# Layer 0 begins on a scale-only input: x transposed on the host, the shift added afterwards

## The chip, the cores and the metric

The kernel runs on one core of one Trainium2 chip. The metric is the time of one execution on the device in microseconds; the time given for a kernel is the median over its runs. A profile is one execution recorded by the hardware profiler, with every instruction's start and end.

## The reference

Two layers of a mixer that serves a context pass (128 rows, conditioned by `c_ctx`) and a denoising step (512 rows, conditioned by `c`) with the same weights. All data are float32. The part that matters here:

```
def layer_step(x, cvec, p, ...):
    shift, scale, gate = split(silu(cvec) @ w_ada + b_ada, 3)      # w_ada: 2048 x 6144
    h = rms_norm(x, norm_g) * (1.0 + scale) + shift                # x: 128 or 512 rows of 2048
    aq, ak, av, ag, bq, bff, bfb, bi, bg, cu, cv, cg = split_proj(h @ w_in)   # w_in: 2048 x 6656
    a_out = windowed attention of aq, ak, av (QK norm, rotary positions) * silu(ag)
    b_out = two gated linear recurrences (HGRN) of bq, bff, bfb, bi, normed * silu(bg)
    c_out = cu * (position mixing of layer-normed cv) * silu(cg)
    y = concat(a_out, b_out, c_out) @ w_out                        # 2048 x 2048
    return x + gate * y, ...
```

Returned are the final x of both passes, the context keys and values of each layer and the final states of the recurrences.

## The kernel before, in words

The 640 rows (128 of context, then 512 of the sample) make five row tiles (NT = 5), the 2048 columns sixteen slices k (KT = 16). For the big products h lies transposed in SBUF: for each k a tile of 128 columns of h by 640 rows. To multiply float32 exactly enough in the fast format, each operand is split into a high part and a rest (`hh`, `hl` for h, `wh`, `wl` for weights; ScalarE copies the high part, VectorE subtracts), and three matmuls per pair of tiles are added up in PSUM: wh with hh, wl with hh, wh with hl (L426 to L428 in row products, L443 in column products).

`rowmajor` makes 512 columns of `h @ W` for all five row tiles: for each k it loads 128 x 512 of W, splits it, and issues 15 matmuls of 512 columns into five PSUM banks (240 in all). `colmajor` makes 128 columns, transposed: for each k six matmuls, three of 384 and three of 256 rows (96 in all). A layer has five row products of `w_in` (AK with AV, AQ, AQ+512, BI, CV), 32 column products (BFF, BFB, BQ, BG, four each, AG eight, CU and CG four each) and four row products of `w_out`.

Side work hangs on the products. `tick()` advances the generators in `self.side` (key and query preparation, attention, recurrence, SGU) by one step between matmuls; `fill()` advances `ada_gen`, which makes the remaining w_ada columns on VectorE (two L286 operations per step) while the products run, at 1.25 steps a group in layer 0. A scheduler orders each engine's instructions ahead of time by a priority, which is the place in the program; what is issued under `hi()` counts as 3000 places earlier. Loads of weights go through SP's queue, x and most small loads through ScalarE's.

Layer 0 begins like this: x comes in rows through ScalarE's queue (`load_x`), ScalarE squares it for the norm (L354), `scale_x` multiplies it by the reciprocal root (L372, L374), and `make_h` transposes it on TensorE (L381, L386), applies scale and shift on VectorE (L388, L390) and splits it. Scale and shift of layer 0 come from `ada_first`, in four blocks of four k's: for each block, w_ada's 512 shift columns and 512 scale columns (8 MB) are loaded, thin matmuls with the two conditioning vectors (L242, 32 columns of weights side by side in four column groups) make them as rows, and small matmuls turn the rows into columns (L254). The first block comes ahead of the AK product; the other three are made during it, four k's ahead of their use.

Of the kernel before, what the change touches and what calls it, by code (L numbers as in the profile page):

```python
# [8 lines left out]
F32 = mybir.dt.float32  # L9
# [4 lines left out]
ALU = mybir.AluOpType  # L14
# [28 lines left out]
def host_consts():  # L43
# [25 lines left out]
    for qd in range(4):  # L69
        for cd in range(2):  # L70
            misc[32 * qd + cd, 248 + 2 * qd + cd] = 1.0
# [5 lines left out]
class Net:  # L77
    def __init__(self, ctx, tc, I, C, O):
        self.tc, self.nc, self.I, self.C, self.O = tc, tc.nc, I, C, O
        self.ctx = ctx  # L80
        self.pools()
        self.uid = 0

# [37 lines left out]

    def hi(self):
        return self.tc.high_priority(offset=HP)

    # ---------------------------------------------------------------- constants
    def setup(self):
# [8 lines left out]
        self.sel8 = misc[:, 248:256]  # L135
# [16 lines left out]
        self.sc = self.g(512).rearrange("p (k c) -> p k c", k=KT)  # L152
        nc.vector.memset(self.sc, 0.0)
        self.s2 = cst.tile([P, KT, 2], F32, name="s2")
        self.ones = cst.tile([P, 32], F32, name="ones")
# [31 lines left out]
    def setup2(self):  # L187
# [25 lines left out]
        self.gd = [self.dr.tile([2, D], F32, name=f"gd{l}", tag=f"gd{l}") for l in range(DEPTH)]  # L213
        self.x1 = [self.dr.tile([P, D], F32, name=f"x1_{t}", tag=f"x1_{t}") for t in range(NT)]
# [7 lines left out]
    # ---------------------------------------------------------------- adaLN  # L222
    def ada_load(self, blk, k, pool):
        raw = []
        with self.hi():
            for s in range(2):
                if pool == "hp":
                    r = self.hp.tile([P, 512], F32, tag=("hh", "hl")[s], name=self.nm("wa"))
                else:
                    r = self.ev(512)  # L230
                c0 = D * s + 512 * blk
                self.nc.sync.dma_start(r, self.I["w_ada"][0, k * P:(k + 1) * P, c0:c0 + 512])
                raw.append(r)
        return raw

    def ada_first(self, blk, pre):
        nc = self.nc
        acc = self.bank()
        for k in range(KT):
            raw = pre[k] if k < len(pre) else self.ada_load(blk, k, "hp")  # L240
            for qd in range(4):
                nc.tensor.matmul(  # L242
                    acc[32 * qd:32 * qd + 32, 0:256],
                    lhsT=self.sc[:, k, :],
                    rhs=raw[qd // 2][:, 256 * (qd % 2):256 * (qd % 2) + 256],
                    start=k == 0, stop=k == KT - 1, skip_group_check=True,
                )
            if k < KT - 1:
                yield
        rows = self.g(256)  # L250
        nc.scalar.activation(rows, acc[:, 0:256], AF.Copy)
        b = self.bank()
        for s in range(2):
            nc.tensor.matmul(b[:, 8 * s:8 * s + 8], lhsT=rows[:, 128 * s:128 * s + 128], rhs=self.sel8,  # L254
                             start=True, stop=True, skip_group_check=True)
        ps = b[:, 0:16].rearrange("p (s q c) -> p q s c", s=2, q=4)
        for qq in range(2):
            k0 = 4 * blk + 2 * qq
            self.mod_cols(0, 0, k0, 2, ps[:, qq])
            self.mod_cols(0, 1, k0, 2, ps[:, 2 + qq])  # L260
        yield

# [11 lines left out]
    def ada_steps(self, l, blk):  # L274
# [15 lines left out]
        if blk >= 8:  # L290
            for cd in range(2):
                nc.tensor.matmul(b[32 * cd:32 * cd + 32, :], lhsT=self.ones, rhs=acc[:, cd], start=True, stop=True,
                                 skip_group_check=True)
# [47 lines left out]
    # ---------------------------------------------------------------- layer input  # L341
    def load_x(self):
        self.xt = []
        self.ssq = self.small(4 * NT, "ssq")
        for t in range(NT):
            x = self.mg()
            src = self.I["x_prompt"][0] if t == 0 else self.I["x_sample"][0, (t - 1) * P:t * P]
            for c in range(4):
                self.nc.scalar.dma_start(x[:, 512 * c:512 * c + 512], src[:, 512 * c:512 * c + 512])
            self.xt.append(x)  # L350
        for t in range(NT):
            for c in range(4):
                junk = self.ev(512)
                self.nc.scalar.activation(junk, self.xt[t][:, 512 * c:512 * c + 512], AF.Square,  # L354
                                          accum_out=self.ssq[:, 4 * t + c:4 * t + c + 1])
# [43 lines left out]
    # ---------------------------------------------------------------- big products  # L399
    def wload(self, srcs, nk, n):  # L400
        nc = self.nc
        with self.hi():
            raw = self.wrp.tile([P, nk, n], F32, tag="wr", name=self.nm("wr"))
            o = 0
            for s in srcs:
                w = s.shape[1]
                nc.sync.dma_start(raw[:, :, o:o + w], s.rearrange("(a p) n -> p a n", p=P))
                o += w
# [6 lines left out]
    def rowmajor(self, W, c0, hook=None):  # L415
# [3 lines left out]
        for ks in groups:  # L419
            if hook is not None:  # L420
                hook(ks[0])
# [700 lines left out]
```

## Time and profile before

| what | value |
|---|---|
| median of three runs | 2324.17 us (2321.46 to 2326.08) |
| span of the profiled execution, first to last instruction | 2323.5 us |
| TensorE matmuls busy | 2230.3 us (96%) |
| VectorE busy | 1387.9 us (60%) |
| ScalarE busy | 763.2 us (33%) |
| GpSimd busy | 308.2 us (13%) |
| mean granted TensorE clock | 0.988 |
| moved by DMA | 283.70 MB, mean 122 GB/s |

The profiled execution has no time of its own besides its span, which is what the views are measured against; it stands 0.7 us under the median. "Busy" of TensorE is the union of its matmuls' records; these overlap, as the next begins before the one before has ended, so the distance between their starts says more than their length. Line numbers (L426) are those of the kernel before. A plain float32 matmul shows as two records.

### The profile page before, as it was taken

The numbers are of one execution on the slowest core, as the hardware profiler recorded it, in microseconds if no ns is written. First come the engines' busy times: TensorE is split into PE (matmuls) and PEld (weight loads), VectorE is DVE, ScalarE is ACT, GpSimd is POOL, SyncE is SP. The second block draws the span as 40 slices with busy tenths as digits, with TensorE's granted clock in tenths as the row PEclk, the third lists the DMA queues.
The fourth block names the chain that finished last, engine by engine and source line by source line (L and its number), as shares of the span: only waits on it lengthen the run. The fifth ranks groups of instructions, "written<-read, shape, count | busy, mean of one in ns | idle before, by whom it ended". The sixth has DMA issues, their size and how long they took to land.

```text
span 2323.5 us, 35038 instructions
## 1 busy us (share of the span) xinstructions
PE 2230.3 (96%) x13362; PEld 1960.9 (84%) x13362; DVE 1387.9 (60%) x2570; ACT 763.2 (33%) x1593; POOL 308.2 (13%) x242
## 2 busy tenths in 40 slices
PE   3999999999999999999999999999999999999999
PEld 1668778989989989988887878799999998998887
DVE  2367797688988768652236456855865942434232
ACT  4232344434333322242224234344343332223111
POOL 0011010022222101011112010101222310100110
PEclk9999999999999999999999999999999999999999
DMA  9864333344443555543332221322422423324332
GB/s 345 316 195 124 111 101 109 112 120 134 133 124 114 172 166 147 151 158 109 109 118 73 77 60 50 116 60 72 124 82 75 122 88 92 100 78 150 105 109 82
DMA packets 255612, 283.70 MB, mean 122 GB/s; under 512 B 17586, under 2 KB 156740, under 8 KB 254164
## 3 DMA queue, kind: packets, MB, share of 16 engines
q1 hardware_dynamic: 243664, 256.59, 35.7%
q10 hardware_dynamic: 11780, 24.88, 3.3%
q8 instruction: 105, 1.72, 0.3%
q14 instruction: 63, 0.52, 0.1%
HBM read 269.30 MB, written 12.09 MB: 121 GB/s over the span
## 4 chain that ended last, share of the span: by engine, by line
PE 80%; DVE 11%; DMA 5%; issue 2%; ACT 1%; POOL 0%; SPq 0%; DVEq 0%; ACTq 0%; POOLq 0%
PE m L443 32%; PE m L426 13%; PE m L427 13%; PE m L428 12%; DMA wa<-in_w_ada_dram 4%; DVE aacc L286 3%; DVE wl L412 2%; PE s L621 1%; PE s L667 1%; PE s L242 1%; DMA wr<-in_w_in_dram 1%; PE s L831 1%; PE s L679 1%; DVE g L507 1%; DVE g L508 1%
## 5 line engine op out<-in xcount | busy, mean ns | idle before, releaser
L412 DVE TENSOR_TENSOR wl<-wr,wh 128x512 fp32r<-128x512 f32 x544 | 404.6, 745 | 620.2 <-ACT wh L411 613.5
L411 ACT ACTIVATE wh<-wr 128x512 fp32r<-128x512 f32 x544 | 342.0, 630 | 967.3 <-PE m L428 528.7
L426 PE MATMUL m<-wh,hh 128*128 128x512 f32 x1440 | 568.6, 395 | 0.4 <-DVE vT L464 0.2
L427 PE MATMUL m<-wl,hh 128*128 128x512 f32 x1440 | 566.0, 393 | 0.7 <-DVE wl L412 0.7
L428 PE MATMUL m<-wh,hl 128*128 128x512 f32 x1440 | 565.0, 393 | 0.0
L443 PE MATMUL m<-hh,wh 128*128 128x384 f32 (+1 forms) x2048 | 482.8, 317 | 0.0
L443 PE MATMUL m<-hl,wh 128*128 128x384 f32 (+1 forms) x2048 | 469.5, 310 | 0.0
L443 PE MATMUL m<-hh,wl 128*128 128x384 f32 (+1 forms) x2048 | 469.0, 310 | 0.2 <-DVE wl L412 0.2
L286 DVE SCALAR_TENSOR_TENSOR aacc<-wa,s,aacc 128x512 f32<-128x512 f32 x480 | 369.2, 800 | 60.7 <-DMA wa<-in_w_ada_dram 58.8
L426 PEld LDWEIGHTS m<-wh,hh 128*128 128x128 f32 x1440 | 272.1, 189 | 61.2 <-issue 5.0
L443 PEld LDWEIGHTS m<-hh,wh 128*128 128x128 f32 x2048 | 316.1, 190 | 7.5 <-issue 5.2
L428 PEld LDWEIGHTS m<-wh,hl 128*128 128x128 f32 x1440 | 271.7, 189 | 55.3 <-issue 0.5
L427 PEld LDWEIGHTS m<-wl,hh 128*128 128x128 f32 x1440 | 272.2, 189 | 54.7 <-DVE wl L412 1.1
L443 PEld LDWEIGHTS m<-hl,wh 128*128 128x128 f32 x2048 | 314.9, 189 | 0.0
L443 PEld LDWEIGHTS m<-hh,wl 128*128 128x128 f32 x2048 | 314.4, 189 | 0.6 <-DVE wl L412 0.4
L816 POOL TENSOR_TENSOR mg<-ev,Dt 128x512 f32<-128x512 f32 x80 | 103.5, 1310 | 338.9 <-PE s L831 129.5
L985 POOL TENSOR_TENSOR mg<-mg,ev 128x512 f32<-128x512 f32 x30 | 41.2, 1374 | 282.6 <-DVE ev L983 279.9
L510 POOL TENSOR_TENSOR mg<-g,g 128x256 f32<-128x256 f32 x32 | 31.9, 1021 | 292.4 <-DVE g L508 292.4
L242 PE MATMUL s<-wa,g 128*32 128x256 f32 x464 | 40.8, 433 | 24.4 <-DMA wa<-in_w_ada_dram 22.6
L651 ACT ACTIVATE g<-g,st,qs 128x384 f32<-128x384 f32 (+1 forms) x64 | 48.0, 752 | 37.1 <-DVE st L647 37.1
L242 PEld LDWEIGHTS s<-wa,g 128*32 128x32 f32 x464 | 14.1, 117 | 49.3 <-DMA wa<-in_w_ada_dram 39.6
L667 PE MATMUL s<-misc,g 128*128 128x128 f32 x240 | 41.7, 283 | 13.8 <-DVE g L656 13.4
(225 smaller groups left out, 1866.7 us busy)
## 6 DMA issues: line engine op xcount, KB each, us to landing
wr<-in_w_in_dram SPq DMA_DIRECT2D x416, 256.0 KB, 2.9
wa<-in_w_ada_dram SPq DMA_DIRECT2D x372, 256.0 KB, 3.0
wr<-in_w_out_dram SPq DMA_DIRECT2D x128, 256.0 KB, 2.9
x<-mg SPq DMA_DIRECT2D x20, 256.0 KB, 2.4
mg<-x ACTq DMA_DIRECT2D x5, 1024.0 KB
out_dram<-mg SPq DMA_DIRECT2D x20, 256.0 KB, 2.7
mg<-in_x_sample_dram ACTq DMA_DIRECT2D x16, 256.0 KB, 5.4
g<-gd ACTq DMA_DIRECT2D x16, 256.0 KB, 4.9
```

Of the source, the lines that this page charges most:

```text
L242: nc.tensor.matmul(acc[32 * qd:32 * qd + 32, 0:256], lhsT=self.sc[:, k, :], rhs=raw[qd // 2][:, 256 * (qd % 2):256 * (qd % 2) + 256], star ...
L286: nc.vector.scalar_tensor_tensor(acc[:, cd], r, sc, acc[:, cd], op0=ALU.mult, op1=ALU.add)
L411: nc.scalar.activation(wh, raw, AF.Copy)
L412: nc.vector.tensor_tensor(wl, raw, wh.bitcast(F32), op=ALU.subtract)
L426: nc.tensor.matmul(ps[t], lhsT=hh, rhs=wh[:, 0], start=k == 0, stop=False)
L427: nc.tensor.matmul(ps[t], lhsT=hh, rhs=wl[:, 0], start=False, stop=False)
L428: nc.tensor.matmul(ps[t], lhsT=hl, rhs=wh[:, 0], start=False, stop=k == KT - 1)
L443: nc.tensor.matmul(ps[hf][:, 0:n], lhsT=w[:, a], rhs=h[:, o:o + n], start=k == 0 and i == 0, stop=k == KT - 1 and i == 2)
L651: nc.scalar.activation(dst[h], src[h], AF.Exp, bias=nmx[:, h:h + 1], scale=rq[:, h:h + 1], accum_out=den[:, h:h + 1])
L667: nc.tensor.transpose(pb[:, h * P:(h + 1) * P], dst[h][:, kb * P:(kb + 1) * P], self.ident)
L816: nc.gpsimd.tensor_tensor(k.rearrange("p (i c s) -> p i c s", i=4, c=4), bc(c4(pre[d][0])[:, j], 1, 4), bc(dd, 3, 32), op=ALU.mult)
L985: (nc.vector if c == 3 else nc.gpsimd).tensor_tensor(xs, xs, y, op=ALU.add)
```

## The change

The host also passes x transposed (`xT`: 128 x 16 x 640), and layer 0 gets a beginning of its own, `begin`. It runs the first three row products in three rounds.

* `first_round`: x comes in four transfers of four k's through SP's queue; `first_norm` squares it on ScalarE, sums over k by matmuls with a 128 x 128 matrix of ones, makes the reciprocal root, and multiplies the four x tiles by it in place on VectorE. Then AK and the first column product of CU are made from h with scale only (`scaled_h`). The scale columns of w_ada come in five chunks of k (4, 4, 4, 2, 2), each made by thin matmuls (`rows_mm`, with k's spread over four column groups) during the chunk before. The results without shift stay in SBUF (`kraw`, `cu0`).
* `second_round`: the AQ product, still without shift, while the shift columns of w_ada are made as rows (`shift_rows`); from k = 8 on, `shift_h` adds the shift to the first eight k's of h and splits them again.
* In `begin`, outside `hi()`: the AQ+512 product, with `shift_h` for the other eight k's. Beside it `bias_rows` makes shift times W for the AK, AQ and first CU columns by thin matmuls on W loaded once more, spreads the rows over 128 partitions by matmuls with a selector, and adds them to `kraw`, the AQ result and `cu0`; only then do `kav_post` and `q_post` go on, and the key preparation and first attention steps enter `side`.

After BI the other three CU products and the first CG product of layer 0 are made, ahead of the B group; their results (`cud`) wait in DRAM and are read back after the flush at the end of the layer. Layer 1 goes on as before. The same change makes a `hi()` inside another one do nothing, and splits `wload` into `wraw` and `wsplit`, with `mm_row` and `mm_col` as helpers.

```diff
+    def first_norm(self, xm):
+        b = [self.bank(), self.bank()]
+        for k in range(KT):
+            s = self.g()
+            nc.scalar.activation(s, xm[k // 4][:, k % 4], AF.Square)
+            for hf, (o, n) in enumerate(HALF):
+                nc.tensor.matmul(b[hf][:, 0:n], lhsT=self.ones, rhs=s[:, o:o + n], start=k == 0, stop=k == KT - 1)
+        r = self.g()
+        for hf, (o, n) in enumerate(HALF):
+            nc.scalar.activation(r[:, o:o + n], b[hf][:, 0:n], AF.Ln, bias=self.bias[:, 0:1], scale=1.0 / D)
+        nc.scalar.activation(r, r, AF.Exp, scale=-0.5)
+        for m in xm:
+            nc.vector.tensor_tensor(m, m, bc(r, 1, 4), op=ALU.mult)
+
+    def rows_mm(self, acc, lhs, kk, rhs, n):
+        q = kk % 4
+        self.nc.tensor.matmul(acc[32 * q:32 * q + 32, 0:n], lhsT=lhs[:, kk, :], rhs=rhs, start=kk < 4, stop=kk >= 12,
+                              skip_group_check=True)
+
+    def scaled_h(self, k, x):
...
+        for cd, a, b in self.SEG:
+            gs = self.gs[:, 0, k, cd:cd + 1]
+            nc.scalar.activation(hh[:, a:b], x[:, a:b], AF.Copy, scale=gs)
+            nc.vector.scalar_tensor_tensor(hl[:, a:b], x[:, a:b], gs, hh[:, a:b].bitcast(F32),
+                                           op0=ALU.mult, op1=ALU.subtract)
+
+    def shift_h(self, k):
+        hh, hl = self.hh[k], self.hl[k]
+        t = self.g()
+        for cd, a, b in self.SEG:
+            nc.vector.scalar_tensor_tensor(t[:, a:b], hh[:, a:b].bitcast(F32), self.sh[:, 0, k, cd:cd + 1],
+                                           hl[:, a:b].bitcast(F32), op0=ALU.add, op1=ALU.add)
+        nc.scalar.activation(hh, t, AF.Copy)
+        nc.vector.tensor_tensor(hl, t, hh.bitcast(F32), op=ALU.subtract)
+
+    def first_round(self, W):
+        for i in range(4):
+            m = self.mg().rearrange("p (k t) -> p k t", k=4)
+            nc.sync.dma_start(m, self.C["xT"][:, 4 * i:4 * i + 4, :])
...
+        sc[0] = load_scale(0)
+        w[0] = load_w(0)
+        self.first_norm(xm)
+        sc[1] = load_scale(1)
+        for kk in range(KT):
+            self.rows_mm(acc, self.sc, kk, sc[0][kk], 512)
+        rows = self.rows_copy(acc, 512)
+        self.mod_cols(0, 1, 0, 4, self.rows_cols(acc, rows, 512))
...
+            for k in ks:
+                x = self.wsplit(raw[k - k0], 1, 512)
+                self.scaled_h(k, xm[k // 4][:, k % 4])
+                for t in range(NT):
+                    self.mm_row(ps[t], t, k, x)
+                for kk in range(m * (k - k0), m * (k - k0 + 1)):
+                    self.rows_mm(acc, self.sc, kk, sc[ci + 1][kk], nn * P)
+            rows = self.rows_copy(acc, nn * P)
+            for k in ks:
+                if k == k0 + nk // 2:
+                    b = self.rows_cols(acc, rows, nn * P)
+                    self.mod_cols(0, 1, k0 + nk, nn, b)
+                self.mm_col(pc, k, cw, k - k0)
...
+    def second_round(self, W):
+        steps = self.shift_rows()
+        def hook(k):
+            for _ in range(1 + k % 2):
+                next(steps, None)
+            if k >= 8:
+                self.shift_h(k - 8)
+        ps = self.rowmajor(W, AQ, hook)
...
+    def bias_rows(self, W):
+        def spread(rows, dst):
+            for cd in range(2):
+                nc.tensor.matmul(b[cd], lhsT=wide[:, cd], rhs=rows, start=True, stop=True)
+            for t in range(NT):
+                nc.vector.tensor_tensor(dst[t], dst[t], b[min(t, 1)], op=ALU.add)
...
+        yield from self.rows_block(shp, W[:, AK:AK + 512], 512, kav)
+        yield from self.rows_block(shp, W[:, AQ:AQ + 512], 512, aq)
+        yield from self.rows_block(shp, W[:, CU:CU + P], P, cu)
...
+    def begin(self, W):
+        with self.hi():
+            self.setup()
+            self.first_round(W)
+            self.second_round(W)
+        self.setup2()
+        self.prep_ctx(0)
+        self.filler = self.ada_gen([(0, b) for b in range(8, 12)] + [(1, b) for b in range(8)])
+        self.fill_rate = 1.25
+        steps = self.bias_rows(W)
+        def hook(k):
+            if k < 8:
+                self.shift_h(k + 8)
+            if k:
+                next(steps, None)
+        ps = self.rowmajor(W, AQ + 512, hook)
...
         self.bi_evac(self.rowmajor(W, BI))
+        if l == 0:
+            for h in range(1, 4):
+                self.cu_evac(h, self.colmajor(W, CU + h * P))
+            u = self.g()
+            nc.scalar.dma_start(u, self.cud[0])
+            self.mul_evac(self.colmajor(W, CG), u.rearrange("p (t q) -> p t q", q=P), True, nc.vector)
+            nc.scalar.dma_start(self.cud[0], u)
```

More of the change, by code (lines that the diff above doesn't have):

```diff
@@ L220, in sigma @@
         nc.scalar.activation(t, t, AF.Exp, scale=-1.0)
[L223 to L234, printed above, removed]
@@ L237, in ada_first, with rows_cols, rows_block @@
+    def rows_cols(self, acc, rows, n):
+        b = acc[:, 0:n // P * 2].rearrange("p (s c) -> p s c", c=2)
+        for i in range(n // P):
+            self.nc.tensor.matmul(b[:, i], lhsT=rows[:, i * P:(i + 1) * P], rhs=self.sel, start=True, stop=True,
+                                  skip_group_check=True)
+        return b
+    def rows_block(self, lhs, src, n, done):
         nc = self.nc
         acc = self.bank()
[L239 to L260, printed above, removed]
@@ L261, in ada_first, with shift_rows @@
-        yield
+        m = 2048 // n
+        for k0 in range(0, KT, m):
+            with self.hi():
+                raw = self.mgp.tile([P, m, n], F32, tag="mg", name=self.nm("wa"))
+                nc.sync.dma_start(raw, src[k0 * P:(k0 + m) * P].rearrange("(a p) n -> p a n", p=P))
+            for a in range(m):
+                self.rows_mm(acc, lhs, k0 + a, raw[:, a], n)
+            yield
+        rows = self.rows_copy(acc, n)
+        yield
+        done(acc, rows)
+        yield
+    def shift_rows(self):
+        for c in range(4):
+            yield from self.rows_block(
+                self.sc, self.I["w_ada"][0, :, 512 * c:512 * c + 512], 512,
+                lambda acc, rows: self.mod_cols(0, 0, 4 * c, 4, self.rows_cols(acc, rows, 512)))
@@ L339, in flush @@
             self.tick()
-    def load_x(self):
-        self.xt = []
-        self.ssq = self.small(4 * NT, "ssq")
-        for t in range(NT):
[L346 to L350, printed above, removed]
-        for t in range(NT):
[L352 to L355, printed above, removed]
+    SEG = ((0, 0, P), (1, P, T))
@@ new lines, in second_round @@
+    def second_round(self, W):
+        nc = self.nc
+        steps = self.shift_rows()
[5 more added lines that the diff above has]
+        ps = self.rowmajor(W, AQ, hook)
+        for _ in steps:
+            pass
+        self.A[0] = A = self.mg()
+        for t in range(NT):
+            a = A[:, 512 * t:512 * t + 512]
+            if t % 2:
+                nc.vector.tensor_copy(a, ps[t])
+            else:
+                nc.scalar.activation(a, ps[t], AF.Copy)
@@ L993, in out_proj, with begin_next @@
         self.xt, self.ssq = xt, ssq
-    def layer(self, l):
-        W = self.I["w_in"][l]
-        self.hh, self.hl = [], []
-        self.A, self.rq = {}, {}
+    def begin(self, W):
+        with self.hi():
+            self.setup()
[12 more added lines that the diff above has]
+        ps = self.rowmajor(W, AQ + 512, hook)
+        for _ in steps:
+            pass
+        self.q_evac(0, 1, ps)
+    def begin_next(self, l, W):
         self.norm_x()
```

319 lines of the change are left out of this document (237 added, 82 removed).

## The prediction

> **What bounds the kernel now.** I read the page's head and slices first, then stretches between the starts of the big products, then the waits and the timeline of TensorE.
>
> ```profile
> span 2323.5 us, 35038 instructions
> PE 2230.3 (96%) x13362; PEld 1960.9 (84%) x13362; DVE 1387.9 (60%) x2570; ACT 763.2 (33%) x1593; POOL 308.2 (13%) x242
> PE   3999999999999999999999999999999999999999
> DMA  9864333344443555543332221322422423324332
> ```
>
> TensorE is busy from the second slice (58 us each) to the end; the one slice with room is the first, where DMA is full. The profiled span is 0.7 us under the median of the three runs, 2324.17; the sum below is made against the span, and 0.7 us added at the end. No difference under 0.2% (4.6 us) can be told from no change.
>
> ```profile
> core 0: us, PE busy (x) PEld busy (x) DVE busy (x) ACT busy (x) POOL busy (x), PEclk, DMA share, GB/s
> 0.00:65.20 65.20, 28.70 (x267) 11.54 (x267) 18.13 (x59) 25.05 (x70) 4.00 (x10) 0.95 0.97 349
> 65.20:157.50 92.30, 86.29 (x588) 60.62 (x587) 43.10 (x89) 21.94 (x42) 10.10 (x6) 1.00 0.79 270
> 157.50:216.00 58.50, 57.82 (x257) 45.49 (x255) 42.15 (x93) 18.16 (x43) 4.42 (x8) 1.00 0.44 131
> 216.00:303.50 87.50, 83.00 (x401) 65.68 (x400) 70.52 (x150) 34.47 (x78) 7.92 (x8) 0.96 0.35 101
> 303.50:392.60 89.10, 84.67 (x401) 66.48 (x401) 72.99 (x152) 33.98 (x77) 9.43 (x8) 0.98 0.35 104
> 392.60:451.20 58.60, 57.73 (x387) 56.04 (x386) 41.34 (x84) 22.76 (x49) 0.00 (x0) 1.00 0.40 119
> ...
> 157.50:216.00 58.50, 31.88 (x80) 15.02 (x80) 1.00 0.44 131
> ```
>
> The stretches are: before the first product, then the layer-0 products AK, AQ, AQ+512, BI, and the first three column products. The last row, of line 426 alone, shows how they were cut: AQ's stretch holds 80 of its matmuls, a third of one row product.
>
> ```profile
> PE s L242 <- DMA wa<-in_w_ada_dram: 22.6, 10, 19.1
> PE s L254 <- ACT g L251: 8.6, 4, 7.0
> ...
> 2.50:20.00 17.50, 1.76 (x6) 0.55 (x6) 2.72 (x18) 1.14 (x4) 0.00 (x0) 1.00 0.96 330
> ```
>
> Up to 65 us TensorE waits for w_ada (22.6 us), then for ScalarE (8.6 us). Transfers run at 330 to 349 GB/s with DMA 96% busy: the start is bound by bytes, 5.2 MB of x and 8.4 MB of w_ada ahead of the first h.
>
> **Prices.** All later steps use these rows.
>
> ```profile
> 70.32 0.39 PE L427 MATMUL m<-wl,hh 128*128 128x512 f32 x1
> 70.54 0.39 PE L428 MATMUL m<-wh,hl 128*128 128x512 f32 x1
> 70.77 0.39 PE L426 MATMUL m<-wh,hh 128*128 128x512 f32 x1
> ...
> 794.73 0.46 PE L443 MATMUL m<-hh,wh 128*128 128x384 f32 x2
> 797.08 0.46 PE L443 MATMUL m<-hh,wl 128*128 128x384 f32 x2
> ...
> 116.86 1.93 PE L242 MATMUL s<-wa,g 128*32 128x256 f32 x32
> 118.73 0.50 PE L426 MATMUL m<-wh,hh 128*128 128x512 f32 x1
> ...
> 81.06 0.63 PE L381 MATMUL s<-misc,mg 128*128 128x128 f32 x4
> 81.53 1.04 PE L386 MATMUL s<-misc,mg 128*128 128x128 f32 x8
> ...
> 27.57 1.08 PE L242 MATMUL s<-wa,g 128*32 128x256 f32 x8 [19.09 <-DMA wa<-in_w_ada_dram]
> 79.02 1.07 PE L242 MATMUL s<-wa,g 128*32 128x256 f32 x16
> ```
>
> Starts of matmuls are what counts, since they overlap. A row matmul starts every 0.227 us: 240 make 54.5 us a row product. A column pair (384 and 256 columns) takes 2.35/8 = 0.294 us: 48 make 14.1 us. Thin fp32 matmuls (32 columns of weights, four side by side): 32 records of 256 columns in 1.87 us, so 16 k's of 512 columns cost 2 x 1.87 = 3.75 us. Full-width plain fp32: 4 records in 0.47 us, two to a matmul, so 0.235 us per 128 columns. The last two rows show TensorE at half speed after idleness: 8 records in the time of 16.
>
> ```profile
> L412 DVE TENSOR_TENSOR wl<-wr,wh 128x512 fp32r<-128x512 f32 x544 | 404.6, 745 | 620.2 <-ACT wh L411 613.5 <-DMA wr<-in_w_in_dram 2.7 <-DMA wr<-in_w_out_dram 2.7
> L286 DVE SCALAR_TENSOR_TENSOR aacc<-wa,s,aacc 128x512 f32<-128x512 f32 x480 | 369.2, 800 | 60.7 <-DMA wa<-in_w_ada_dram 58.8
> L395 DVE TENSOR_TENSOR hl<-g,hh 128x640 fp32r<-128x640 f32 x16 | 14.3, 898 | 0.0
> L983 DVE TENSOR_TENSOR ev<-m,g 128x512 f32<-128x512 f32 x40 | 27.6, 690 | 15.9 <-PE m L428 15.4
> L374 DVE TENSOR_SCALAR mg<-mg,rr 128x512 f32<-128x512 f32 x24 | 9.8, 482 | 0.3 <-ACT rr L364 0.3
> L394 ACT ACTIVATE hh<-g 128x640 fp32r<-128x640 f32 x16 | 11.8, 736 | 16.3 <-DVE g L390 11.4 <-DMA snk<-in_attn_sink_dram 3.9 <-DMA g<-const_tri_dram 1.0
> ```
>
> **The start.** Removed: the x rows in ScalarE's queue, their squares and scalings, and 80 transposes (80 x 0.235 = 18.8 us of TensorE, 3.8 of them ahead of the first product). Added: x transposed, first in SP's queue (four transfers of 1.31 MB), `first_norm`, and only the scale columns of w_ada, 4.2 MB. SP's queue then holds W of chunk 0 and the next scale chunk; nothing else waits behind x, since ScalarE's queue has only setup's small loads.
>
> ```profile
> 2.12 0.41 SPq L144 DMA_DIRECT2D g<-in_c_dram  x1
> 4.80 0.31 ACT L149 ACTIVATE g<-g 32x128 f32<-32x128 f32 x1 [2.79 <-DMA g<-in_c_dram]
> ...
> L933 DVE TENSOR_TENSOR mg<-mg,m 128x384 f32<-128x384 f32 x32 | 17.5, 547 | 9.3 <-PE m L443 9.3
> L933 DVE TENSOR_TENSOR mg<-mg,m 128x256 f32<-128x256 f32 x32 | 13.2, 414 | 0.0
> ```
>
> The chain: SP issues x at about 2.6 us, after three small loads, of which the last is used 2.3 us after its issue ended. 1.31 MB at 330 GB/s is 4.0 us; with 2 us of latency (estimate, a little under those 2.3) the first quarter of x is there at 8.5 us. A square like L394, 0.74: 9.3. The ones-matmuls, 16 k's of 640 columns, 16 x 5 x 0.235 = 18.8 us, go slower than x arrives (four k's: 4.7 us against 4.0); with 2 us for the half-speed beginning (bounds 0 and 4) they end at 30.1. Three activations make r: about 2 us, 32.1. Then come the four multiplications by r, of 2560 elements each. No row has that size; L933's two sizes give 133 ns for 128 elements more, so 2560 take 0.414 + 18 x 0.133 = 2.8 us, 11.2 in all. The lower end is five L374 pieces, 2.4 us each time, the upper one four L395 pieces, 3.6. The Trainium skill (VectorE: DVE Perf Modes, The perf-mode tier table) speaks against this form of scaling: an fp32 operation on two SBUF tensors has no double-rate mode, one with a scalar has. Its 2.29 us for 2048 elements give an estimate of 2.87 here, 11.5 in all, and a sum longer by 0.3 us; had the scaling kept L374's form, it would be 9.6 and the sum shorter by 1.6. The trace agrees: 482 ns against 745 for 512 elements.
> They stand ahead of the scale columns and of the first split in program order, and in this kernel such work does go first:
>
> ```profile
> 44.92 3.77 ACT L372 ACTIVATE mg<-mg,rr 128x512 f32<-128x512 f32 x6
> 49.20 0.36 ACT L251 ACTIVATE g<-s 128x256 f32<-128x256 f32 x1
> 49.62 1.02 PE L254 MATMUL s<-misc,g 128*128 128x8 f32 x4 [7.04 <-ACT g L251]
> ```
>
> So VectorE is free at 43.3, and with the scale columns and the first split (1.2 us) the first product starts at **44.5 us** against 65.2. If only the first multiplication is waited for, 36; with the dear ends (14.4 for the multiplications, 4 for the half speed), 50. Bytes don't bind: x, first scale chunk and W are 10.7 MB, 32 us at 330 GB/s.
>
> **First round.** AK 54.5, column product CU0 14.1 (moved here), three scale chunks' worth of thin matmuls 11.2, their 12 small turning matmuls (two records of 0.11 us each, as L381) 2.7, a half-speed restart after some 9 us of idleness 2, four boundaries where rows become columns and then h, hidden by CU0's matmuls but for about 2: 86.5 us, to 131. Loads are 22 MB after x, 67 us at 330 GB/s, so TensorE binds. VectorE needs per k a split (0.75) and hl (1.1) in over 4 us: hidden.
> **Second round.** AQ 54.5, shift rows 4 x 3.75 = 15.0, turning 3.6, rest 0.5: 73.6, to **204.6**. Its 21 MB take 64 us at that rate. `shift_h` goes on from k = 8, 2 us on VectorE and 0.74 on ScalarE per k, hidden.
> Before, the third product starts at 216.0: 11.4 us won. By then CU0 is done too: another 14.1 won, when its column product falls away later.
> **Third product.** AQ+512 now carries the bias rows: 3.75 for AK, 3.75 for AQ, 0.9 for CU, spreading with four full fp32 matmuls of 512 columns 4 x 4 x 0.235 = 3.8, turning 0.3: 12.5 us more of TensorE. k's preparation moves here from AQ's stretch, where it and its waits made 58.5 - 54.5 = 4.0 us. Its extra 9.4 MB of weights are read beside a DMA that is 35% busy: nothing, and if a load were late, rows wait behind it on TensorE.
> VectorE is the question. In this stretch it gets 16 splits (11.9), 15 fills of 1.25 ada steps of two L286 (30), 8 `shift_h` (8 x 2.05 = 16.4), ten additions of bias (6.9), q_post and q_evac (20 operations of L983's size, 13.8), q's rope (16 of 256 elements, 6.6), and some 45 small ones for k and v (0.3 each, an estimate under L933's 0.41, 14): 99 us beside 71 us of TensorE. Some 28 us slip. The next stretches had 17.0, 16.1 and 17.3 us of VectorE idle, so they can take it; splits are marked urgent and go ahead. Bounds 0 and 28; I take 2, under the 4.3 us that TensorE stood idle in ten of the fullest on VectorE before:
>
> ```profile
> 230.00:240.00 10.00, 5.73 (x25) 4.42 (x24) 9.80 (x23) 3.11 (x11) 2.27 (x2) 0.90 0.54 161
> ```
>
> **Later.** Attention starts a product later, and CU1 to CU3 and CG0 stand before the B group to carry it; the same matmuls in another order: 0. u goes to DRAM and back in ScalarE's queue, with four more multiplications (0.9 each, as L395) after the flush, covered by CG3's 14.1 us: 1 us (0 to 5).
> **Sum:** -11.4 - 14.1 + 12.5 + 4.0 + 2 + 1 = -6.0 us: span 2317.5, with 0.7 added **2318**. With the start's and the unknown ends: about 2309 to 2327.
>
> **Rivals.**
> *The multiplications don't block* (the scheduler puts scale columns and first split between them, as VectorE has only 0.4 + 0.75 + 1.1 us of them): start at 36 instead of 44.5, restart without idleness, 8.5 to 11 us less, 2307, and to 2295 if shorter idleness also spares the half-speed stretches. For it: the scale rows have landed by then. Against: L251's 7 us behind L372.
> *VectorE becomes the bound in the third product* and ends on the other side. It decides if the order fixed beforehand puts ada steps in front of splits: a split that is late by one 0.8 us step stops TensorE for as long. Without my 2 us for it the sum is -8.0; the change is slower by over 0.2% from 12.6 of the 28 us on TensorE, and at 20 to 28 the time is 2336 to 2344. For it: the ten microseconds shown, 98% of VectorE and 4.3 us of TensorE idle. Against: 16 to 17 us of VectorE idle in each stretch behind.
> *The start isn't shortened*: loads of later constants (some 1.3 MB) in ScalarE's queue, now free of x, and scale tiles that wait for buffers put the first product at 55 to 60: 2329 to 2334. For it: DMA 79% busy up to 157 us. Against: TensorE's ones-matmuls, not bytes, are the longer chain.
>
> **How the numbers follow.** Forecast 0.45 (of it 0.25 faster, 0.18 same, 0.02 slower, as 2319.5 cuts its range); no blocking 0.26, all faster; VectorE bound 0.22, slower; start not shortened 0.07 (0.03 same, 0.04 slower). Faster 0.51, same 0.21, slower 0.28. The forecast's own range is 2309 to 2327; to hold 8 in 10 it must take in most of the first two rivals: 2295 to 2340.
>
> **What would show it.** The first matmul of a product at 44.5 us with four long multiplications just before; the second and third product's starts at 131 and 205; no DMA waits of TensorE between; the third product's stretch about 73 us with VectorE near full, longer if the second rival holds; column products of layer 0 numbering 31 after it. A first product after 50, or a third stretch over 85 us, would make the prediction wrong.

## The result, and the profile after

| kernel | median of runs, us | lowest to highest, us | profiled span, us |
|---|---|---|---|
| before | 2322.82 (4 runs beside those of the changed kernel) | 2319.0 to 2326.08 | 2323.5 |
| changed | 2357.52 (4 runs) | 2351.92 to 2361.55 | 2355.6 |

The changed kernel is slower: ratio 1.0145, 95% interval 1.0126 to 1.0164. The profiled spans differ by 32.1 us. The forecast was 2318.

The head and three of the slice rows of the profile page of the changed kernel:

```profile
span 2355.6 us, 34870 instructions
PE 2258.8 (96%) x13276; PEld 1969.0 (84%) x13276; DVE 1414.7 (60%) x2605; ACT 782.5 (33%) x1603; POOL 290.0 (12%) x234
PE   4999999999999989989999999999999999999999
DMA  8556733444444355555332221322332423324332
```

The first slice is as thin as before (4 against 3), though x is no longer transposed on TensorE. Stretches tell more. A row has the stretch and its length, the busy time of TensorE, weight loads, VectorE, ScalarE and GpSimd with the number of their instructions, then the granted clock, DMA share and GB/s. The cuts are the starts of the products AK, AQ, AQ+512, BI, the first column product behind BI, CV, the first row product of `w_out`, and the second; the last row is the three products of `w_out` behind the first, up to layer 1's first. First the changed kernel:

```profile
0.00:67.90 67.90, 30.74 (x146) 17.86 (x146) 18.03 (x37) 18.39 (x31) 0.66 (x8) 0.99 0.91 324
67.90:154.90 87.00, 86.71 (x457) 65.19 (x457) 31.50 (x61) 30.38 (x59) 0.00 (x0) 0.96 0.46 144
154.90:230.40 75.50, 75.50 (x398) 50.73 (x395) 28.39 (x54) 19.60 (x30) 0.00 (x0) 1.00 0.66 225
230.40:306.50 76.10, 73.87 (x360) 49.99 (x359) 64.48 (x136) 27.94 (x63) 3.86 (x8) 1.00 0.70 232
306.50:392.00 85.50, 81.26 (x382) 62.79 (x381) 72.57 (x148) 30.11 (x68) 7.95 (x8) 0.96 0.38 115
392.00:913.50 521.50, 500.75 (x3610) 478.09 (x3609) 433.33 (x803) 195.58 (x427) 91.87 (x67) 0.99 0.44 131
913.50:1019.90 106.40, 105.44 (x606) 95.82 (x605) 85.98 (x134) 35.80 (x66) 15.73 (x10) 1.00 0.52 156
1019.90:1091.30 71.40, 61.79 (x258) 49.63 (x257) 50.03 (x76) 15.81 (x28) 5.88 (x5) 0.93 0.60 203
1091.30:1264.10 172.80, 167.05 (x738) 137.32 (x736) 55.27 (x92) 50.50 (x105) 16.64 (x12) 0.98 0.35 113
```

The same view of the kernel before, from its first column product on (its earlier stretches stand in the prediction):

```profile
392.60:825.50 432.90, 413.78 (x3047) 399.28 (x3046) 358.65 (x634) 154.41 (x337) 85.13 (x59) 0.98 0.44 132
825.50:1002.90 177.40, 177.40 (x1102) 167.97 (x1101) 130.23 (x210) 49.23 (x88) 14.77 (x10) 1.00 0.52 156
1002.90:1057.40 54.50, 54.50 (x243) 45.12 (x242) 21.37 (x29) 17.02 (x30) 6.95 (x6) 1.00 0.42 141
1057.40:1230.10 172.70, 166.93 (x737) 137.25 (x735) 55.25 (x92) 50.43 (x105) 16.62 (x12) 0.98 0.35 113
```

So the 32.1 us have four addends: first product +2.7 (67.9 against 65.2); from there to the first `w_out` product +14.3 (952.0 against 937.7); that product +16.9 (71.4 against 54.5); all behind it -1.8. The second is as forecast: 9.3 more for the first two rounds (160.1 forecast, 150.8 before) and -14.1 + 12.5 + 4.0 + 2 make 13.7. Only this total can be compared: with the attention beginning a product later, side work left the third product (401 matmul records before, 360 now) and went into the column products. **The forecast failed at two places:** a first product 23.4 us late, and a `w_out` product 15.9 us longer than the 1 us given to it.

**The start.** The changed kernel's timeline, rows of ScalarE, TensorE and VectorE in order of time (start, length, instruction, and in brackets idle time before it and what ended it):

```profile
18.21 0.21 ACT L181 ACTIVATE g<-g 128x16 f32<-128x16 f32 x1 [1.89 <-DVE g L180]
33.47 0.63 ACT L621 ACTIVATE wh<-wr 128x512 fp32r<-128x512 f32 x1 [15.04 <-DMA wr<-in_w_in_dram]
34.00 2.60 ACT L366 ACTIVATE g<-mg 128x640 f32<-128x640 f32 x4
34.77 20.01 PE L368 MATMUL s<-g,ones 128*128 128x384 f32 x64 [17.39 <-ACT g L366]
56.13 11.03 DVE L374 TENSOR_TENSOR mg<-mg,g 128x2560 f32<-128x2560 f32 x4 [15.81 <-ACT g L372]
67.08 0.23 DVE L287 SCALAR_TENSOR_TENSOR gs<-s,cols 128x8 f32<-128x8 f32 x2
67.93 0.79 PE L633 MATMUL m<-wh,hh 128*128 128x512 f32 x1 [2.35 <-ACT hh L383]
```

ScalarE stands still for 15 us in front of an instruction of another chain: the split of W's first tile (L621), whose load is queued behind x and 16 scale tiles. The squares (L366), whose first quarter of x should have been there at 8.5 us, come behind it and start at 34.0. From there the forecast chain runs in its forecast lengths: ones-matmuls 20.0 us (20.8 said), multiplications 11.0 (11.2 said). The first h then needs the scale columns (`gs`, L287), whose matmuls end at 60.2, but VectorE makes the columns only behind all four multiplications: these do block here.

**The first `w_out` product.** Its waits on TensorE (who waits for what: us in total, times, longest):

```profile
PE m L633 <- DVE mg L1188: 4.2, 1, 4.2
PE m L634 <- DVE wl L622: 3.1, 2, 2.3
PE s L319 <- DVE aacc L302: 2.3, 1, 2.3
```

Three rows of VectorE's timeline in it:

```profile
1022.12 3.75 DVE L1209 TENSOR_TENSOR hl<-mg,hh 128x640 fp32r<-128x640 f32 x5
1025.80 0.87 DVE L1188 TENSOR_TENSOR mg<-mg,m 128x384 f32<-128x384 f32 x2
...
1027.73 2.73 DVE L302 SCALAR_TENSOR_TENSOR aacc<-wa,s,aacc 128x512 f32<-128x512 f32 x4
```

VectorE serves three things in turn there: the splits of the mixer's output (`split_mix`, L1209), what is left of the last column product (L1188, which frees a PSUM bank that TensorE waits for), and ada steps (L302, two operations to a step). The waits come to 9.6 of the 16.9 us. The rest goes to TensorE at half speed behind them (granted clock 0.93 in the stretch, 1.00 before) and to 15 matmul records more than before (258 against 243). The ada operations by stretch (VectorE alone, that line alone): changed kernel from the second product, then before's second and first `w_out` product.

```profile
154.90:230.40 75.50, 0.00 (x0) 1.00 0.66 225
230.40:1019.90 789.50, 267.89 (x354) 0.99 0.47 143
1019.90:1091.30 71.40, 26.83 (x37) 0.93 0.60 203
```

```profile
157.50:216.00 58.50, 15.96 (x22) 1.00 0.44 131
1002.90:1057.40 54.50, 0.00 (x0) 1.00 0.42 141
```

The second product carried 22 of these operations before, and the first product 8 (7.1 us). Now neither carries any, since the filler is set behind them, and 37 are left beside `split_mix`.

### The profile page after: what moved, and what is told of

It is laid out like the page before. It is cut to its first block, busy times and chain, and to the rows that moved or that the text cites. A ratio compares the mean times of both kernels' runs of the same rounds, so it can differ in the third digit from the quotient of the medians.

```text
span 2355.6 us, 34870 instructions
## 1 busy us (share of the span) xinstructions
PE 2258.8 (96%) x13276; PEld 1969.0 (84%) x13276; DVE 1414.7 (60%) x2605; ACT 782.5 (33%) x1603; POOL 290.0 (12%) x234
## 5 line engine op out<-in xcount | busy, mean ns | idle before, releaser
L622 DVE TENSOR_TENSOR wl<-wr,wh 128x512 fp32r<-128x512 f32 (+1 forms) x535 | 404.1, 757 | 628.6 <-ACT wh L621 619.7
L621 ACT ACTIVATE wh<-wr 128x512 fp32r<-128x512 f32 (+1 forms) x535 | 336.1, 629 | 953.8 <-PE m L635 542.2
L641 PE MATMUL m<-hh,wh 128*128 128x384 f32 x2016 | 478.2, 317 | 1.8 <-ACT g L1350 1.8
L641 PE MATMUL m<-hl,wh 128*128 128x384 f32 x2016 | 463.1, 310 | 0.0
L641 PE MATMUL m<-hh,wl 128*128 128x384 f32 x2016 | 462.6, 310 | 0.0
L302 DVE SCALAR_TENSOR_TENSOR aacc<-wa,s,aacc 128x512 f32<-128x512 f32 x480 | 364.3, 791 | 61.2 <-DMA wa<-in_w_ada_dram 60.0
L1240 POOL TENSOR_TENSOR mg<-mg,ev 128x512 f32<-128x512 f32 x30 | 41.2, 1372 | 288.2 <-DVE ev L1238 284.2
L228 ACT ACTIVATE ev<-ev 128x640 f32<-128x640 f32 x40 | 29.5, 738 | 65.6 <-DVE ev L227 64.4
L926 DVE TENSOR_TENSOR g<-s,g 128x512 fp32r<-128x512 f32 x56 | 38.4, 688 | 20.6 <-ACT g L925 15.0
```

The costliest lines, as they stand in the source:

```text
L302: nc.vector.scalar_tensor_tensor(acc[:, cd], r, sc, acc[:, cd], op0=ALU.mult, op1=ALU.add)
L621: nc.scalar.activation(wh, raw, AF.Copy)
L622: nc.vector.tensor_tensor(wl, raw, wh.bitcast(F32), op=ALU.subtract)
L641: self.nc.tensor.matmul(ps[hf][:, 0:n], lhsT=w[:, a], rhs=h[:, o:o + n], start=k == 0 and i == 0, stop=k == KT - 1 and i == 2)
L926: nc.vector.tensor_tensor(pt[1], pb, pt[0].bitcast(F32), op=ALU.subtract)
L1240: (nc.vector if c == 3 else nc.gpsimd).tensor_tensor(xs, xs, y, op=ALU.add)
```

## The experiments

The table has, from the matmul starts in each trace, the start of the first product, the stretch from AK to AQ, the column products behind BI up to CV, the first `w_out` product (O1), the three behind it, and the span; then the median of the runs and the ratio to the kernel before.

| kernel | first product | AK to AQ | columns | O1 | O2 to O4 | span | median | ratio, 95% interval |
|---|---|---|---|---|---|---|---|---|
| changed | 67.9 | 86.9 | 521.5 | 71.4 | 172.7 | 2355.6 | 2357.5 | 1.0145 (1.0126 to 1.0164) |
| e1 | 51.3 | 86.2 | 519.3 | 69.8 | 172.7 | 2334.5 | 2338.0 | 1.0055 (1.0038 to 1.0072) |
| e2 | 50.5 | 84.6 | 521.3 | 69.4 | 172.7 | 2332.4 | 2335.8 | 1.0043 (1.0028 to 1.0058) |
| e3 | 66.6 | 86.4 | 567.6 | 54.4 | 172.8 | 2370.7 | 2375.4 | 1.0214 (1.0198 to 1.0229) |
| e4 | 67.3 | 86.5 | 521.5 | 67.4 | 172.7 | 2364.2 | 2367.8 | 1.0185 (1.0166 to 1.0204) |
| e5 | 68.5 | 86.9 | 521.8 | 54.4 | 181.0 | 2342.7 | 2344.9 | 1.0092 (1.0077 to 1.0107) |
| e6 | 50.9 | 93.1 | 521.6 | 67.2 | 172.7 | 2340.5 | 2340.4 | 1.0075 (1.006 to 1.009) |
| e7 | 46.3 | 102.9 | 519.2 | 71.2 | 172.7 | 2351.1 | 2350.7 | 1.0119 (1.0102 to 1.0136) |
| e8 | 45.6 | 102.6 | 507.7 | 54.4 | 185.7 | 2324.7 | 2326.9 | 1.0028 (1.0014 to 1.0042) |
| e9 | 50.7 | 85.5 | 521.0 | 70.1 | 172.7 | 2332.1 | 2336.4 | 1.0055 (1.0038 to 1.0073) |
| e10 | 41.3 | 92.9 | 520.6 | 67.1 | 172.7 | 2329.1 | 2331.4 | 1.0038 (1.0026 to 1.005) |
| e11 | 40.4 | 92.5 | 521.5 | 54.4 | 181.5 | 2318.1 | 2321.4 | 0.9999 (0.9987 to 1.001) |
| e12 | 41.2 | 93.2 | 533.5 | 58.0 | 172.7 | 2327.7 | 2328.5 | 1.0017 (1.0007 to 1.0026) |
| e13 | 41.2 | 92.9 | 513.8 | 54.4 | 183.9 | 2316.3 | 2316.1 | 0.996 (0.9946 to 0.9973) |
| e14 | 40.8 | 92.5 | 525.0 | 54.4 | 202.9 | 2342.4 | 2346.7 | 1.0094 (1.008 to 1.0107) |

**e1: squares first.**

```
 for k in range(KT):                       # first_norm
-    s = self.g()
+    s = self.ev()
     nc.scalar.activation(s, xm[k // 4][:, k % 4], AF.Square)
```

> The changed kernel with one word changed: the tile that takes a square comes from the five buffers of pool ev instead of the seven of pool g. Order theory (ScalarE's fixed order had the split of W's first tile ahead of the squares because the setup's tiles still held pool g when the order was laid out): the squares start at about 8 us instead of 34.0. TensorE's ones-matmuls then wait only for the setup's transpose (L166, 16.7 us), end near 37.5 instead of 54.8; between them and the four multiplications stand 3.75 us of thin matmuls and a row copy, so the first product starts at 50 to 55 us instead of 67.9, nothing later changes: 13 to 18 us less, 2340 to 2345. Rival (the size of the x transfers, or bytes, hold the start): the squares do not move or wait for x, first product after 64, 2354 to 2358.

The start in e1:

```profile
8.38 1.36 ACT L366 ACTIVATE ev<-mg 128x640 f32<-128x640 f32 x2 [6.36 <-issue]
12.44 20.31 PE L368 MATMUL s<-ev,ones 128*128 128x384 f32 x64
33.60 0.63 ACT L621 ACTIVATE wh<-wr 128x512 fp32r<-128x512 f32 x1 [5.40 <-DMA wr<-in_w_in_dram]
36.96 0.73 ACT L372 ACTIVATE g<-g 128x640 f32<-128x640 f32 x1
38.57 11.02 DVE L374 TENSOR_TENSOR mg<-mg,g 128x2560 f32<-128x2560 f32 x4
38.87 10.80 PE L240 MATMUL s<-wa,pad 128*32 128x512 f32 x32 [0.70 <-DMA wa<-in_w_ada_dram]
51.27 0.47 PE L633 MATMUL m<-wh,hh 128*128 128x512 f32 x1
```

One word moves the squares to 8.4 us and the first product by 16.6 to 51.3; the transfers of x are issued as before, within 0.2 us. The order theory is shown, the rival falls; the median, 2338.0, is 2 us under the expected range. That taking the squares' tiles from pool g held them back is shown too, as nothing else changes; that its seven tiles were still held by the setup's when the order was laid out is argued from the code. The forecast 44.5 is still missed by 6.8: r comes at 37.7 instead of 32.1, since the split of W (its load lands at 33.6) and the row copy of the first scale chunk still stand ahead of its steps; then the multiplications end at 49.6. And the second scale chunk's thin matmuls (L240), which the program has behind the first h's products, stand ahead of the first product: they take 10.8 us, up to 49.7, as their weights come in (the first chunk's took 3.6).

**e2: the setup's wait.** `nsnk`, the negated sink (L220), goes from VectorE to GpSimd on top of e1.

> As e1, and the negation of the attention sink (L220), which stood first in VectorE's queue behind a DMA that landed at 15.35 us, goes to GpSimd. Theory: the setup chain on VectorE and ScalarE runs as soon as c has landed (9 us), L166 starts at about 10.5 instead of 16.7, the ones-matmuls end near 31, the first split of W (its load landed at 33.4) is then the later of the two, and the first product starts at 47 to 49: 4 to 6 us less than e1, 18 to 21 less than the changed kernel, 2337 to 2340. Rival (in e1 TensorE waits for squares or x, not for the setup): as e1 within 1 us.

First product 50.5, 0.8 earlier, within the rival's 1 us. The theory was wrong: in e1 the sink had landed at 10.0 us, not at 15.4 as in the changed kernel, and the setup's transpose ran at 12.0 in both.

**e3 and e4: what makes O1 long.** e3 changes `fill_rate` in `begin` from 1.25 to 1.5; e4 drops the early CG0 and computes it behind the last flush:

```
-self.mul_evac(self.colmajor(W, CG), u..., True, nc.vector)      # ahead of the B products
...
-for h in range(1 - min(l, 1), 4):
+for h in ((1, 2, 0, 3) if l == 0 else range(4)):
     self.mul_evac(ps[h] if h in ps else self.colmajor(W, CG + h * P), self.view(self.Cm, h), True, nc.vector)
```

> The changed kernel with the fill rate of layer 0 raised from 1.25 to 1.5 ada steps a place, nothing else. Theory A (the first product of out_proj, 71.4 us against 54.4, is long because ada steps are still queued on VectorE beside split_mix): the ada steps end before the last column products, the first out_proj product takes 55 to 59 us, 10 to 16 us less in all, 2341 to 2348, less up to 4 us for a fuller VectorE in the stretches behind the second product. Theory B (only one column product, 14 us, is left behind the flush to cover split_mix): the ada steps end earlier but the product keeps 66 to 72 us, and the time stays within 5 us of 2357.

> The changed kernel with the column product CG0 put back behind the last flush (four multiplications of C by u as before, then CG0 and CG3 instead of CG3 alone), fill rate 1.25. Theory B (cover): the first out_proj product takes 55 to 60 us instead of 71.4, 10 to 16 us less, 2341 to 2348; what CG0 carried of attention ahead of the B products moves elsewhere at no cost. Theory A (ada steps on VectorE): they end at about the same time, some 14 us more of TensorE work stands in front, the product keeps 64 us or more, and the time is 2350 to 2357.

Both totals were missed: both kernels got slower. By parts: with the ada steps done earlier (e3) O1 is back at 54.4, but the column products take 46 us longer. In e4, 14 us more cover (TensorE work between the last flush and O1, under which VectorE prepares O1's operands) take only 4.0 us off O1, which keeps 67.4 and 38 ada operations; and the early stretches gain nothing from the column product taken out (columns 521.5, with one product fewer). So O1 is long mainly for the ada steps, and CG0 ahead of B had cost nothing.

**e5: the ada steps pause.** `self.fill_rate = 0.0` ahead of CG1, `0.5` after the first `w_out` product.

> The changed kernel; the ada steps pause (fill rate 0) from the column product CG1 to the end of the first out_proj product and go on at 0.5 in the three out_proj products behind, where VectorE was busy 14.5 of 54.4 us. Some 20 of 216 steps move. Theory (the first out_proj product is long because ada steps share VectorE with split_mix there): that product takes 54 to 58 us instead of 71.4, the three behind stay at 54.4, nothing else changes: 13 to 17 us less, 2340 to 2345. Rival (what is left of cover behind the flush is too short for split_mix, whatever else VectorE does): 66 us or more, 2351 to 2357. Raising the rate to 1.5 had brought that product to 54.4, but lengthened the stretch of column products by 46 us.

O1 and the three products behind it in e5:

```profile
1017.50:1071.90 54.40, 54.40 (x243) 45.06 (x242) 21.32 (x29) 16.99 (x30) 6.87 (x6) 1.00 0.41 141
1071.90:1252.90 181.00, 172.30 (x774) 142.30 (x772) 88.07 (x147) 50.78 (x106) 16.64 (x12) 0.98 0.45 143
```

17.0 us come back in O1 and 8.3 are paid behind it; with some 4 us from other stretches it is 12.9 less in all, and the median, 2344.9, is in the expected range. That the ada steps make O1 long is shown. The pause also empties VectorE ahead of O1, from CG1 on, so the steps beside O1 and those just ahead of it are not told apart. That the steps would cost nothing later was wrong.

**e6 and e7: the multiplications, with GpSimd.** On e2, three of the four multiplications go to GpSimd (`(nc.gpsimd if i else nc.vector).tensor_tensor(...)`); e7 adds 0 times hh of k = 0 to the scale rows' operand ahead of the second chunk.

> As e2, but only the first of the four multiplications by r stays on VectorE, the other three go to GpSimd. Theory (in the fixed order the thin matmuls of the second scale chunk and its row copy stand ahead of the first product, and they waited for its load until 48.9 us in e2, when the fourth multiplication also ended): the first product stays at 49 to 50.5 us, 2333 to 2337 in all. Rival, the prediction's step (the four multiplications hold the first product): it starts at 41 to 43, 8 us less, 2326 to 2329.

> As e6, and the thin matmuls of the second scale chunk are made to wait for the first h: the scale rows' left operand gets 0 times hh of k = 0 added (one VectorE operation of 512 elements). Theory (the second chunk's load and the multiplications each held the first product until 49 us, so only both together free it): first product at 41 to 43 us, the first round as long as before, 7 to 9 us less than e2: 2325 to 2329. Rival (bytes: the chunk's weights are late wherever the matmuls stand): TensorE waits in them after the first k, and CU0 starts no earlier than in e2 (64.7): 2333 to 2337.

In e6 the first product stayed at 50.9, as the theory said, but the span rose by 8 us; e7, at 2350.7, came out 22 us above its theory's range. The reason is a third thing (e6's timeline, VectorE and GpSimd):

```profile
38.32 4.90 DVE L288 TENSOR_TENSOR gs<-gs,cols 128x8 f32<-128x8 f32 x1
45.88 12.06 DVE L622 TENSOR_TENSOR wl<-wr,wh 128x512 fp32r<-128x512 f32 x2
37.60 19.80 POOL L374 TENSOR_TENSOR mg<-mg,g 128x2560 f32<-128x2560 f32 x3 [27.15 <-ACT g L372]
```

Two splits that take 1.3 us together took 12.1, until GpSimd was done. The second part of the first h (`hl`) comes behind them, and AK to AQ is 93.1 and 102.9. Neither kernel tests what it was made for.

**e8: the sum of the ends.** e7 with a rate of 1.0 instead of 1.25, the pause, and 1.35 behind O1.

> e7 together with a pause as in e5 and a fill rate of 1.0 instead of 1.25 ahead of it, 1.35 in the last three out_proj products (some 59 ada steps move there). If the two ends add up: 2326 less 15 is 2311, and the lower rate shortens the stretch of column products by up to 15 us (it got 46 us longer with 1.5): 2296 to 2313. If VectorE becomes the limit in the out_proj products (20 steps of 1.6 us each and 14.5 us of their own, 46 of 54.4 us): those get longer, 2313 to 2325.

Columns 507.7, O1 54.4, the three behind it 13 us longer: the parts are as expected, but they had been counted from 2326 for e7, which took 2350.7. Span 2324.7, and the median 1.0028 of the kernel before.

**e9 and e10: the two holders of the first product, without GpSimd.** On e1; e9 has the first and last pair of lines, e10 all:

```
 self.scaled_h(k, xm[k // 4][:, k % 4])
+if k == 0:                                    # e10 alone
+    self.after_h(self.sc..., 512, k)          # sc = 0 * hh[k] + sc, on VectorE
+if k in (0, 2, 4):
+    self.after_h(self.rn, T, k)               # r = 0 * hh[k] + r
+    self.norm_chunk(xm[k // 2 + 1])           # a multiplication by r
```

> e1 (squares from pool ev) with only the first of the four multiplications by r ahead of the first product, all four on VectorE: the other three are tied to hh of k = 0, 2 and 4 (r gets 0 times hh added, 0.9 us each). GpSimd is left alone: in e6 and e7 VectorE's splits took 12 us beside GpSimd's three long multiplications. Theory (the second scale chunk, whose thin matmuls stand ahead of the first product and whose load lands at 48 to 49 us, holds it as well): first product at 50 to 51 us as in e1 (51.3), 2336 to 2340 in all. Rival, the prediction's step (the multiplications alone hold it): 42 to 44, 2327 to 2331.

> e9, and the second scale chunk's thin matmuls are tied to hh of k = 0 as in e7, again without GpSimd. Theory (two holders of the first product, each until about 49 us, free only together): first product at 42 to 44 us, W-splits of VectorE at 0.7 us each, CU0's column product no later than 58 (67.1 in e1), 7 to 9 us less than e1: 2328 to 2332. Rival (bytes: the second chunk is late wherever its matmuls stand): TensorE waits in them after k = 0 until 49, CU0 at 64 or later, 2335 to 2339.

TensorE in e9, then in e10:

```profile
37.86 11.21 PE L240 MATMUL s<-wa,pad 128*32 128x512 f32 x32 [0.38 <-DMA wa<-in_w_ada_dram]
```

```profile
41.27 0.80 PE L644 MATMUL m<-wh,hh 128*128 128x512 f32 x1 [3.70 <-ACT hh L389]
47.93 1.06 PE L240 MATMUL s<-wa,pad 128*32 128x512 f32 x8
```

The multiplications alone: first product 50.7, nothing won, as the thin matmuls end at 49.1. Both: 41.3. So the thin matmuls held it until 49. No run moves them alone with all four multiplications left on VectorE; that these would then have held `hl`, and with it the third matmul, until about 50 is read from e1, where the last ends at 49.6. But AQ starts at 134.2 against 137.4: only 3.2 of the 10.0 us are kept. The second chunk's thin matmuls (3.6 us) and its turning (1 us) now stand between products instead of in the idle time, and the first 15 matmuls run at half speed (6.7 us to the thin ones, 3.4 at full; in e1 some 8 did). The median is in the expected 2328 to 2332, but the gain on e1 is 6.6 and not 7 to 9, and CU0 comes at 62.8 and not by 58: the expectation had left both out.

**e11: e10 and the pause (1.0 behind it).**

> e10 and the pause of the ada steps as in e5 (rate 1.25 before it), going on at 1.0 behind the first out_proj product, so that none is left for the fourth (in e5 the fourth and layer 1's beginning took 68.7 us instead of 64.0). If the start and the end add up: e10 less 13 to 18 us, 2311 to 2318, below the kernel before (2322). If they do not: 2319 or more.

They do not quite add up: the median is 10.0 us under e10's, not 13 to 18, and at 2321.4 it is no different from the kernel before (0.9999, 0.9987 to 1.001).

**e12: the ada steps back in the second product.** On e10, the filler is set ahead of `second_round`, its weights there in mg tiles.

> e10 with the ada steps begun in the second product again, as in the kernel before (rate 1.25 from there on, no pause; their weights go through the mg tiles there, since the two ar tiles hold the operands of the scale and shift rows). VectorE was busy 28.5 of 75.5 us in that product, DMA 65%; 19 of the 216 steps (1.5 us each) return to it. Theory (the first out_proj product is long because these displaced steps run beside split_mix): it takes 54 to 57 us instead of 67.2, the stretches up to it keep their length, the second product gets 0 to 4 us longer: 9 to 13 less than e10, 2316 to 2323, and none of e11's 8.7 us in the later out_proj products. Rival (it was long for want of cover behind the flush): 65 us or more, 2329 to 2335. If loads of ada steps delay the W tiles: the second product takes over 80 us.

O1 falls from 67.1 to 58.0, with 7 ada operations left in it, and the second product takes 1.1 us more, both about as the theory said; but the span is only 1.4 us under e10's and the median, 2328.5, misses the expected 2316 to 2323, since the column products take 12.9 us longer (BI's stretch got 7.4 shorter, 77.1 against 84.5, so that much may only have moved).

**e13 and e14: the share of the ada steps.** e10 with the pause and rates of 1.0 (1.35 behind O1) and 0.9 (1.7).

> e10 (start) with the ada rate at 1.0 instead of 1.25 up to the pause before CG1, and 1.35 behind the first out_proj product. Theory (ada steps on VectorE hold up the sums and splits that TensorE waits for in the column products): the stretch from the first column product of layer 0 behind BI to CV takes 506 to 510 us instead of 520.6, as in e8, the first out_proj product 54.4 instead of 67.1, the later three 8 to 13 us longer together: 2329.1 less 14, 13 and plus 12, span 2312 to 2317, below the kernel before (2323.5). Rival (the stretch was shorter in e8 for its later start, not for the rate): 518 or more there, 2322 to 2328.

> As e13 with 0.9 and, behind the first out_proj product, 1.7. Theory: the column stretch gets another 2 to 6 us shorter (502 to 506), but 25 steps of 1.5 us in each out_proj product beside its 14.5 us of VectorE are 52 of 54.4 us, and the three take 15 to 30 us longer than 172.7: span 2312 to 2330, no better than e13. Rival (column stretch not set by the ada steps): 518 or more, 2325 to 2340.

e13 is the best version: 0.996 of the kernel before (0.9946 to 0.9973), 0.4% faster. Its columns and the three products behind O1:

```profile
370.20:884.00 513.80, 496.68 (x3579) 474.89 (x3578) 394.09 (x732) 192.50 (x419) 90.41 (x67) 0.99 0.40 119
1041.80:1225.80 184.00, 176.15 (x802) 144.68 (x800) 119.81 (x199) 50.36 (x105) 16.65 (x12) 0.98 0.55 176
```

The column stretch (513.8) lies between theory and rival, though the median is in the theory's range. e14's (525.0) is on the rival's side, and its median, 2346.7, is above both ranges: fewer steps, longer stretch. So the number of steps does not set it alone. One wait in e14's column stretch, some of VectorE's rows in order and then TensorE's:

```profile
575.74 0.75 DVE L302 SCALAR_TENSOR_TENSOR aacc<-wa,s,aacc 128x512 f32<-128x512 f32 x1 [0.22 <-DMA wa<-in_w_ada_dram]
577.06 0.75 DVE L302 SCALAR_TENSOR_TENSOR aacc<-wa,s,aacc 128x512 f32<-128x512 f32 x1
577.73 0.68 DVE L633 TENSOR_TENSOR wl<-wr,wh 128x512 fp32r<-128x512 f32 x1
578.33 0.28 DVE L1102 TENSOR_TENSOR asum<-att,att 128x128 f32<-128x128 f32 x1
...
578.76 0.44 PE L1119 MATMUL s<-misc,asum 128*128 128x128 f32 x1 [6.81 <-DVE asum L1102]
```

TensorE waits 6.8 us for a small sum of the recurrence (`asum`), and ada operations stand ahead of it in VectorE's order. Waits for `asum` in the column stretch come to 21.7 us in e14, 5.7 in e13 and 13.4 in e10: there more of them goes with a longer stretch. They are not all of it: the changed kernel and e3 both have 15.6, at 521.5 and 567.6 us, and e12 has 16.9 at 533.5. Why the order falls out one way at 0.9 and another at 1.0 stays open.

Two things set e13 apart from the kernel before: the new beginning, and the slower ada steps with their pause. No run gives the kernel before the slower steps, and it too has these waits in its column products (before, then e13):

```profile
PE s L853 <- DVE asum L836: 17.9, 11, 5.3
...
PE s L1119 <- DVE asum L1102: 5.7, 5, 2.7
```

With the old rate up to the pause, e11 is even with the kernel before. How much of the 0.4% the new beginning is worth by itself is therefore not shown.

## Why the prediction was wrong

- *"... the first quarter of x is there at 8.5 us. A square like L394, 0.74: 9.3."* **This step failed**, by 24.7 us. x was on time (the first quarter is in by 7.5: the DMA engines stand idle from there to 8.1); the square wasn't next on its engine. The prediction read the program's order as ScalarE's order, and named nothing that waits in front of the squares. e1 gives 8.4 by changing the pool alone.
- *18.8 + 2 us of ones-matmuls; 11.2 us of multiplications ahead of the first product:* right in size (20.0 and 11.0), and right that all four go first. Rival 1 (they don't block, 0.26) fell: in the changed kernel the scale columns come at 67.1, behind all four. But they weren't the only holder: *"Bytes don't bind: x, first scale chunk and W are 10.7 MB"* left out that the second scale chunk, 4.2 MB more, is also ahead of the first product (e9, e10). This is the same fault as the first, an order taken from the program. With the squares' order mended the chain gives 51.3, not 44.5.
- *First round 86.5, second 73.6, third 73:* 87.0, 75.5, 76.1, within 6 us together. The first is partly luck: its 86.5 hold three scale chunks' worth of thin matmuls, but the changed kernel has one of them ahead of the round. Where all three lie in it (e10) it takes 92.9.
- *VectorE in the third product: 28 us of slip, "so they can take it", 2 us.* VectorE was busy 64.5 of 76.1 us there, not with 99 us of work (ada operations took 19.2 us of the 30 counted), and TensorE stood idle 2.2 us: the 2 us came true, its working did not. Rival 2 (VectorE the bound of the third product, 2336 to 2344) named the right engine at the wrong place. The prediction never asked where the ada steps of the first two products go. They had 23 us of VectorE there, and come out at the other end of the layer.
- *Later: "covered by CG3's 14.1 us: 1 us (0 to 5)."* **The second step that failed**: 16.9 us in O1. It priced the moved multiplications and not the queue they stand in; e5 and e3 show the ada steps as the cause, e4 that 14 us more cover buy only 4.0.
- Rival 3 (start not shortened, 0.07) came nearest to what happened at the start, with another mechanism and too low a price (55 to 60).

Sum: -6.0 forecast, + 23.4 (start) + 15.9 (O1) + 0.6 (between) - 1.8 (behind) = 32.1.

## What to carry to other kernels

Where a scheduler fixes each engine's order ahead of time, a chain is only as early as its first instruction's place in that order, and the pool that its tile is taken from can decide that an instruction of another chain, with a late load, stands in front of it. Before a chain is priced, list for each engine on it what stands ahead and which load that waits for. And background work that a change pushes out of one stage has to be followed to where it comes out: VectorE, busy 60% on the average, had no room exactly where its results were waited for.

## What was not expected of the hardware

GpSimd and VectorE held each other up: with three multiplications of 2560 elements on GpSimd (19.8 us), two VectorE splits that take 1.28 us took 12.06, and a product over 8 columns (L288) 4.90 instead of 0.17, while L287, with one operand in PSUM, kept its 0.17. GpSimd was held in its turn: the first of its three multiplications took 5.59 us, the second, into which a multiplication of VectorE's (2.81 us) fell, 8.27. The Trainium skill (SBUF — State Buffer, Who interferes with whom) states it: a VectorE instruction with two SBUF inputs and a GpSimd instruction that reads SBUF exclude each other for the whole instruction. The trace agrees.
